# Scratch writes on SyncE's queue, later uses, single softmax steps and a fifth raw weight tile in a decoder trunk

## The chip, the core and the metric

The kernel runs on one core of one Trainium2 chip. The core has TensorE (PE, the matmuls), VectorE (DVE), ScalarE (ACT), GpSimd (POOL) and SyncE (SP), which here only issues transfers; sixteen DMA engines move data between the chip's DRAM and the core's memory. The metric is the device time of one execution in microseconds (us).

## The reference, cut to what matters

Four decoder layers with three kinds of token mixer in turn (layer 0 and 3: latent attention, layer 1: sparse attention with an indexer, layer 2: a window of 128 tokens with sinks), one row of 256 tokens, width 2048, all in float32. Every layer has one input projection, four memory cross-attention heads, a SiLU gate and one output projection:

```
def reference(x, mem, norm_in, final_norm, mem_norm, rel_bias, w_in_a, ...):
    mem_n = _rmsnorm(mem, mem_norm)
    for i in range(DEPTH):
        h = _rmsnorm(x, norm_in[i])
        kind, j = i % N_MIXERS, i // N_MIXERS
        if kind == 0:
            self_out, mq, gate = _mla_branch(h, w_in_a[j], a_q_norm[j], w_uq[j], a_kv_norm[j], w_ukv[j])
        elif kind == 1:
            self_out, mq, gate = _dsa_branch(h, w_in_b[j], rel_bias)
        else:
            self_out, mq, gate = _swa_branch(h, w_in_c[j], c_sinks[j], rel_bias)
        mem_out = _memory_attention(mq, mem_n @ w_mem_kv[i])
        y = jnp.concatenate([self_out, mem_out], axis=-1) * jax.nn.silu(gate)
        x = x + y @ w_out[i]
    return _rmsnorm(x, final_norm)
```

The latent branch makes queries from a compressed `c_q` (1536 wide, normed) and keys and values from `c_kv` (512 wide, normed); the other two have 32 heads of 64 over 4 key groups, with a relative position bias.

## The kernel before

**Weights.** Each matrix product is done as three float32r products, with activations and weights each cut into a high and a low part. A weight tile of two row tiles (`stage`, 512 KB, buffer `wr`, WR = 4 of them) is loaded on SP's queue; for each of the two, ACT copies the high part (`wh`, L75) and DVE subtracts (`wl`, L84), with WS = 4 buffers each; then PE runs six matmuls of 512 columns (`rows_by`, L381). Undisturbed that is 1.36 us for one row tile and 2.72 us for a stage; one row tile of 128 rows is called a k-tile below. The program is one long run of such stages.

**The scratch round trip.** An activation that is needed in the other layout goes through DRAM. DVE transposes blocks of the accumulator (`turn_blocks`, L284, tile `et`, or `z` first), `put` (L299) writes `et` to a scratch tensor `turned`, and `get` (L306) reads it back with four transfers into `fa` (the compressed streams), `fq` (queries), `kn` (keys), `pT` (softmax weights) or `gT` (gates). All of these are issued from GpSimd, in its program order. Then ACT cuts the tile into its parts, and DVE does the low ones: `gained` (`fa` to `cT`), `row_parts` (`fq` to `fq`), `exact_parts` (`kn`, `pT`), and the query parts of a key group, `qS`. A group's `pT` goes to PE's `o` (L1197) as it is.

**What sets the order.** `other_work` is called once for each stage: `tick` counts stages, and `after(n, job)` puts a job in n stages later. A read is put in BACK = 3 stages behind its write, a use USE = 9 stages behind it. A scheduler then sets the order on each engine from the program's order and its own model of durations; what is pinned (`keep_in_program_order`) stays in program order. So on ACT a use stands between the `wh` copies of later weights, and ACT takes its queue in order.

**The parts.** `Latent`, `Memory` and `GroupedPart` each work one slice of heads: queries, then softmax steps (`weights`, put in as jobs), then `weighted`, then the gate (`write`, `yt`, `y`). In a `GroupedPart` four softmax steps (half, odd) are put in at stages 1, 3, 5 and 7 behind `queries`, each with two `quarter_softmax`, and the bias tile `bm` is loaded at the part's start. In the last layer `split_ahead` cuts a piece of the last output weights ahead of time: 16 pieces of 256 columns, each loaded to `hl` (L1332), cut by ACT (L1342) and DVE (L1343) and written to scratch `sw` (L1346), pinned, on GpSimd's queue, two `hl` tiles in turn.

## Time and profile before

| | us |
|---|---|
| median of 3 runs | 2554.52 (2554.26 to 2557.95) |
| the profiled execution | 2558.04 |
| its span on the core | 2556.1 |
| PE busy | 2498.3 (98%) |
| DVE busy | 1853.7 (73%) |
| ACT busy | 1520.6 (59%) |
| POOL busy | 569.1 (22%) |

Engines' shares are of the span. A row of the timeline gives the start, the busy time, engine, line, operation, output and input tile, shape, how many in a row, and in brackets how long the engine was idle before and what ended that. A row of the waits gives, for one kind of instruction and one releaser, the idle time in total, how many times, and the longest. A row of the windows gives, for a stretch of the span, its length and then each engine's busy time, the granted TensorE clock as a share of its full speed, the share of the DMA engines and GB/s. A DMA issue row gives what is moved, whose queue, how many, the size and the median time from issue to landing.

### The profile page before, as it was taken

Reading aid. Unit: us, or ns where it says so; the run is one execution under the profiler, and the core shown is the slowest. Engines: PE = TensorE matmul, PEld = TensorE weight load, DVE = VectorE, ACT = ScalarE, POOL = GpSimd, SP = SyncE. Lnnn points to the kernel's source line nnn. Section 1 sums busy time; section 2 is a strip of 40 time slices with the busy share of each in tenths; the row PEclk is TensorE's granted clock in tenths of the full one; section 3 lists DMA queues with packets and bytes.
Section 4 is the critical chain, followed back from the end, with each engine's and each line's share of the span. In section 5 each row is a group of like instructions: output and inputs, shape, how many; then the busy total and the mean of one; then the engine's idle time right before and its main releaser. Section 6 shows DMA issues by size and latency. Waiting matters only on the chain. (4 is left out here: it accounts for less than half of the span.)

```text
span 2556.1 us, 37640 instructions
## 1 busy us (share of the span) xinstructions
PE 2498.3 (98%) x11766; PEld 2070.6 (81%) x11766; DVE 1853.7 (73%) x3840; ACT 1520.6 (59%) x3107; POOL 569.1 (22%) x1078
## 2 busy tenths in 40 slices
PE   9999999999999999999999999999999999999998
PEld 7888887787787889887878788878779778888887
DVE  6556555676776687887887776888867567777677
ACT  6555555565565557665666565666656555566564
POOL 3000001133222310123322112222320123432240
PEclk9999999999999999999999999999999999999999
DMA  8787767898879776778878677877875789997994
GB/s 283 250 267 236 235 213 227 233 259 238 228 233 264 236 243 203 222 225 255 276 234 246 200 222 245 253 246 246 245 238 173 224 248 278 267 263 225 269 313 148
DMA packets 404633, 613.96 MB, mean 240 GB/s; under 512 B 80881, under 2 KB 182641, under 8 KB 403793
## 3 DMA queue, kind: packets, MB, share of 16 engines
q1 hardware_dynamic: 347360, 449.71, 58.4%
q0 software_dynamic: 56352, 160.87, 20.3%
q8 instruction: 93, 1.52, 0.2%
q14 instruction: 108, 0.88, 0.1%
q10 hardware_dynamic: 720, 0.98, 0.1%
HBM read 535.83 MB, written 81.89 MB: 242 GB/s over the span
## 5 line engine op out<-in xcount | busy, mean ns | idle before, releaser
L75 ACT ACTIVATE wh<-wr 128x512 fp32r<-128x512 f32 (+1 forms) x1712 | 1046.5, 620 | 774.5 <-DVE wl L84 308.4
L84 DVE TENSOR_TENSOR wl<-wr,wh 128x512 fp32r<-128x512 f32 (+1 forms) x1712 | 1137.8, 676 | 482.7 <-ACT wh L75 473.2
L381 PE MATMUL acc_g<-wh,xT 128*128 128x512 f32 x1536 | 490.6, 394 | 5.3 <-ACT wh L75 5.3
L381 PE MATMUL acc_wo<-wh,y 128*128 128x512 f32 x1504 | 478.5, 393 | 3.6 <-ACT wh L75 3.4
L381 PEld LDWEIGHTS acc_g<-wh,xT 128*128 128x128 f32 x1536 | 290.7, 189 | 67.3 <-ACT wh L75 9.2
L381 PEld LDWEIGHTS acc_wo<-wh,y 128*128 128x128 f32 x1504 | 283.9, 189 | 62.5 <-ACT wh L75 5.6
L381 PE MATMUL acc_g<-wl,xT 128*128 128x512 f32 x768 | 304.6, 397 | 9.1 <-DVE wl L84 8.8
L381 PE MATMUL acc_wo<-wl,y 128*128 128x512 f32 x752 | 296.3, 394 | 2.2 <-DVE wl L84 2.0
L306 POOL DMA_DIRECT2D pT<-turned x320 | 175.0, 554 | 254.2 <-DMA turned<-et 43.1
L299 POOL DMA_DIRECT2D turned<-et x136 | 76.0, 559 | 549.7 <-DVE et L284 482.0
L381 PEld LDWEIGHTS acc_g<-wl,xT 128*128 128x128 f32 x768 | 145.4, 189 | 45.2 <-DVE wl L84 16.1
L381 PEld LDWEIGHTS acc_wo<-wl,y 128*128 128x128 f32 x752 | 142.2, 189 | 32.1 <-DVE wl L84 4.8
L381 PE MATMUL acc_mq<-wh,xT 128*128 128x512 f32 x512 | 162.6, 391 | 0.0
L381 PE MATMUL acc_mk<-wh,mT 128*128 128x512 f32 x512 | 160.4, 392 | 2.2 <-ACT wh L75 2.2
L381 PE MATMUL acc_q<-wh,xT 128*128 128x512 f32 x512 | 159.9, 390 | 0.0
L381 PE MATMUL acc_mv<-wh,mT 128*128 128x512 f32 x512 | 156.4, 389 | 0.9 <-ACT wh L75 0.9
L381 PE MATMUL acc_cq<-wh,xT 128*128 128x512 f32 x384 | 123.9, 402 | 6.4 <-ACT wh L75 6.4
L381 PE MATMUL acc_qn<-wh,cT 128*128 128x512 f32 x384 | 121.4, 392 | 3.5 <-ACT wh L75 3.2
L1367 DVE TENSOR_TENSOR xc<-xc,acc_wo 128x1024 f32<-128x1024 f32 x92 | 111.8, 1215 | 9.0 <-PE acc_wo L381 8.7
L381 PEld LDWEIGHTS acc_mk<-wh,mT 128*128 128x128 f32 x512 | 96.8, 189 | 22.8 <-ACT wh L75 2.6
L381 PEld LDWEIGHTS acc_mv<-wh,mT 128*128 128x128 f32 x512 | 96.0, 188 | 21.1 <-ACT wh L75 1.0
L381 PEld LDWEIGHTS acc_mq<-wh,xT 128*128 128x128 f32 x512 | 96.1, 188 | 19.8 <-ACT wh L75 0.7
(313 smaller groups left out, 3914.4 us busy)
## 6 DMA issues: line engine op xcount, KB each, us to landing
wr<-in_w_out_dram SPq DMA_DIRECT2D x188, 512.0 KB, 4.6
wr<-in_w_in_a_dram SPq DMA_DIRECT2D x176, 512.0 KB, 5.1
wr<-in_w_mem_kv_dram SPq DMA_DIRECT2D x125, 512.0 KB, 4.7
wr<-in_w_in_b_dram SPq DMA_DIRECT2D x116, 512.0 KB, 5.1
wr<-in_w_in_c_dram SPq DMA_DIRECT2D x104, 512.0 KB, 5.1
wr<-in_w_uq_dram SPq DMA_DIRECT2D x144, 256.0 KB, 5.3
turned<-et POOLq DMA_DIRECT2D x104, 256.0 KB, 4.4
wr<-in_w_ukv_dram SPq DMA_DIRECT2D x64, 256.0 KB, 6.0
```

The costliest lines, as they stand in the source:

```text
L75: inst = nc.scalar.activation(o, i, AF.Copy, scale=scale)
L84: nc.vector.tensor_sub(lo, src, f32(hi))
L299: nc.gpsimd.dma_start(d[t].rearrange("i p j n -> (i p) (j n)"), et)
L306: inst = nc.gpsimd.dma_start(dst[32 * j:32 * j + 32].rearrange("p (i n) -> p i n", n=n), d[:, :, :, j, :].rearrange("t i p n -> p (t i) n"))
L381: nc.tensor.matmul(acc[t][:, :n], q[:, v, (s + k) % 4, t * P:(t + 1) * P], w_[:, :n], start=s + k == 0 and v == 0 and w_ is wh, stop=s + k ...
L1367: nc.vector.tensor_add(xs, xs, acc)
```

## The change

1. `put` issues on SP's queue, where the weight loads are, instead of GpSimd's; `get` stays on GpSimd.
2. WR goes from 4 to 5: five raw weight tiles instead of four.
3. USE goes from 9 to 10 stages; for `weighted` there is WAIT = 9; the keys of the memory wait 6 stages as before, by a number of their own.
4. `row_parts` works in two halves, the second a stage later; a group's query parts `qS` are done in two steps, a stage apart; a memory part's second softmax comes 1 stage earlier in its second half (`part` 1).
5. A group's four softmax steps become eight single ones at stages 1, 3, ... 15; its bias load is put in 11 stages later; a memset of `e0` goes from GpSimd to DVE.
6. `split_ahead` takes 32 pieces of 128 columns instead of 16 of 256, each with half the stages between its steps; there are still two `hl` tiles, of half the size. The other users of the old `hl` tile get a `tmp` one.

```diff
--- before.py
+++ after.py
@@ -25,8 +25,8 @@
 MEMW = 1024
 ST = 2
 N_TAB = 384
-PQ, AUX, WR, WS, PT, WARM = 3, 4, 4, 4, 4, 11
-BACK, USE = 3, 9
+PQ, AUX, WR, WS, PT, WARM = 3, 4, 5, 4, 4, 11
+BACK, USE, WAIT = 3, 10, 9


 def _buckets():
@@ -68,8 +68,6 @@
     def f32(ap):
         return ap.bitcast(F32)

-    def part_tile(dt=F32R):
-        return wk.tile([P, 512], dt, name="hl", tag="hl", bufs=2)

     def copy_act(o, i, scale=1.0):
         inst = nc.scalar.activation(o, i, AF.Copy, scale=scale)
@@ -296,7 +294,7 @@
         if d is None:
             d = dr.tile([u, 4, 32, 4, n], F32, name="turned", tag=f"turned{u * n}", bufs=6)
         for t, et in enumerate(ets):
-            nc.gpsimd.dma_start(d[t].rearrange("i p j n -> (i p) (j n)"), et)
+            nc.sync.dma_start(d[t].rearrange("i p j n -> (i p) (j n)"), et)
         return d

     def get(dst, d, pin=None):
@@ -344,8 +342,12 @@
         hi, lo = (act.tile([P, 4, S], F32R, name="fq", tag="pq", bufs=PQ) for v in range(2))
         src = t.rearrange("p u m c -> p m u c")
         h4, l4 = (z.rearrange("p m (u c) -> p m u c", c=32) for z in (hi, lo))
-        copy_act(h4, src)
-        nc.vector.tensor_sub(l4, src, f32(h4))
+
+        def half(m):
+            copy_act(h4[:, m:m + 2], src[:, m:m + 2])
+            nc.vector.tensor_sub(l4[:, m:m + 2], src[:, m:m + 2], f32(h4)[:, m:m + 2])
+        half(0)
+        after(1, lambda: half(2))
         return hi, lo

     def exact_parts(hi, lo):
@@ -704,14 +706,14 @@
                         pin(inst)
                 self.k = act.tile([P, 2, 8, 4, 32], F32R, name="kn", tag="kn", bufs=1)
                 get(flat_of(self.k[:, 1]), mk[i][part], pin)
-                after(USE - BACK, lambda: exact_parts(self.k[:, 0], self.k[:, 1]))
+                after(6, lambda: exact_parts(self.k[:, 0], self.k[:, 1]))
             after(BACK if part == 0 else 11, keys)
             acc = rows_by(nm.at, 16, w, 0, (mq0 + part * 512, 512), "mq")

             def queries(t):
                 self.q = row_parts(t)
                 for h in range(2):
-                    after(1 + 2 * h, lambda h=h: self.weights(h))
+                    after(1 + (2 - part) * h, lambda h=h: self.weights(h))
             features(from_rows(acc), pq_tile, queries)
             gate(nm, w, g0 + 2048 + part * 512, self)

@@ -748,7 +750,7 @@
             def back():
                 pL = weights_tile()[:, :512]
                 get(f32(pL), d)
-                after(USE - BACK, lambda: self.weighted(h, pL))
+                after(WAIT - BACK, lambda: self.weighted(h, pL))
             after(BACK, back)

         def weighted(self, h, pL):
@@ -918,7 +920,7 @@
             def back():
                 pT = weights_tile()
                 get(f32(pT)[:, :384], d)
-                after(USE - BACK, lambda: self.weighted(h, pT))
+                after(WAIT - BACK, lambda: self.weighted(h, pT))
             after(BACK, back)

         def weighted(self, h, pT):
@@ -979,7 +981,7 @@
             s3 = src.rearrange("p (g d) -> p g d", g=n)
             for g0 in range(0, n, 2):
                 m = min(2, n - g0)
-                hl = part_tile()[:].rearrange("p (g v e d) -> p g v e d", g=2, v=2, e=2)
+                hl = tmp("hl", dt=F32R)[:].rearrange("p (g v e d) -> p g v e d", g=2, v=2, e=2)
                 for d in range(2):
                     split(hl[:, :m, 0, d, :], hl[:, :m, 1, d, :], s3[:, g0:g0 + m])
                 transposed(lambda i0, i1: dst(2 * g0 + i0, 2 * g0 + i1),
@@ -1092,16 +1094,19 @@
         def __init__(self, of, g):
             super().__init__()
             self.of, self.g, nm = of, g, of.nm
-            self.bm = bm = act.tile([P, 8, S], F32, name="bm", tag="big3")
             tab = tabs[0 if of.sparse else 1][g]
-            for v in range(2):
-                for e in range(2):
-                    at = 64 * v + 32 * e
-                    nc.gpsimd.dma_start(
-                        bm[at:at + 32, :4],
-                        bass.AP(tensor=tab.tensor,
-                                offset=tab.offset + 4 * e * N_TAB + 63 + 32 * v * (8 * N_TAB - 1),
-                                ap=[[8 * N_TAB - 1, 32], [N_TAB, 4], [1, S]]))
+
+            def biases():
+                self.bm = act.tile([P, 8, S], F32, name="bm", tag="big3")
+                for v in range(2):
+                    for e in range(2):
+                        at = 64 * v + 32 * e
+                        nc.gpsimd.dma_start(
+                            self.bm[at:at + 32, :4],
+                            bass.AP(tensor=tab.tensor,
+                                    offset=tab.offset + 4 * e * N_TAB + 63 + 32 * v * (8 * N_TAB - 1),
+                                    ap=[[8 * N_TAB - 1, 32], [N_TAB, 4], [1, S]]))
+            after(11, biases)
             acc = rows_by(nm.at, 16, of.w, 0, (g * 512, 512), "q")
             ets = []
             for t in range(2):
@@ -1111,22 +1116,25 @@

             def queries(t):
                 self.q = [act.tile([P, 2, 8, 2, 32], F32R, name="qS", tag="pq", bufs=PQ) for z in range(2)]
-                for z in range(2):
+
+                def parts(z):
                     for h, main, low in ((0, slice(0, 64), slice(64, P)), (1, slice(64, P), slice(0, 64))):
                         hi, lo = (self.q[z][rows, h].rearrange("p u j c -> p u (j c)") for rows in (main, low))
                         src = t[main, :, 2 * z:2 * z + 2, :].rearrange("p u j c -> p u (j c)")
                         copy_act(hi, src)
                         nc.vector.tensor_sub(lo, src, f32(hi))
+                parts(0)
+                after(1, lambda: parts(1))
                 while steps:
                     advance()
                 self.pTs = {}
                 self.ets = act.tile([P, 3, 640], F32, name="ets", tag="big2")
-                for n in range(4):
-                    after(1 + 2 * n, lambda n=n: self.weights(n // 2, n % 2))
+                for n in range(8):
+                    after(1 + 2 * n, lambda n=n: self.weights(n // 4, n // 2 % 2, n % 2))
             features(put(ets), pq_tile, queries)
             gate(nm, of.w, of.g0 + g * 512, self)

-        def weights(self, half, odd):
+        def weights(self, half, odd, second):
             of, g, bm, q = self.of, self.g, self.bm, self.q

             def score(r, k0, n):
@@ -1151,20 +1159,25 @@
             flat_et = self.ets[:, (2 * half + odd) % 3]
             et = flat_et.rearrange("p (j m c) -> p j m c", j=4, m=5)
             if of.sparse:
-                e2, e1 = bm[:, 4 + half * 2 + odd, :], ring(P)
-                quarter_softmax(score, bias, ((0, 0, e2[:, 192:]), (1, 0, e1)), None)
-                turn_blocks(et, 0, e1)
+                e2 = bm[:, 4 + half * 2 + odd, :]
+                if not second:
+                    e1 = ring(P)
+                    quarter_softmax(score, bias, ((0, 0, e2[:, 192:]), (1, 0, e1)), None)
+                    turn_blocks(et, 0, e1)
+                    return
                 e3 = ring(S)
                 quarter_softmax(score, bias, ((2, 0, e2[:, :192]), (3, 0, e3)), None)
                 turn_blocks(et, 1, e2, 2)
                 turn_blocks(et, 2, e3, 2)
             else:
                 nsk = nsink[:, u0:u0 + 1]
-                e0, e1 = ring(P), ring(P)
-                nc.gpsimd.memset(e0[:, 64:], 0.0)
-                quarter_softmax(score, bias, ((0, 0, e0[:, :64]), (1, 0, e1)), nsk)
-                turn_blocks(et, 0, e0)
-                turn_blocks(et, 1, e1)
+                if not second:
+                    e0, e1 = ring(P), ring(P)
+                    nc.vector.memset(e0[:, 64:], 0.0)
+                    quarter_softmax(score, bias, ((0, 0, e0[:, :64]), (1, 0, e1)), nsk)
+                    turn_blocks(et, 0, e0)
+                    turn_blocks(et, 1, e1)
+                    return
                 e2 = bm[:, 4 + 2 * odd:6 + 2 * odd, :].rearrange("p a b -> p (a b)")
                 quarter_softmax(score, bias, ((2, 0, e2[:, :192]), (3, 64, e2[:, 192:384])), nsk)
                 turn_blocks(et, 2, e2[:, :3 * P])
@@ -1175,7 +1188,7 @@
                 self.pTs[half, odd] = pT
                 get(flat_of(pT), d)
                 if len(self.pTs) == 4:
-                    after(USE - BACK, self.weighted)
+                    after(WAIT - BACK, self.weighted)
             after(BACK, back)

         def weighted(self):
@@ -1327,24 +1340,26 @@
         pin = tc.keep_in_program_order

         def load(n):
-            q = part_tile()[:].rearrange("p (v c) -> p v c", v=2)
-            k, c0 = part * 4 + n // 2 % 4, 1024 + n // 8 * 512 + n % 2 * S
-            pin(nc.gpsimd.dma_start(f32(q)[:, 1, :], w[k * P:(k + 1) * P, c0:c0 + S]))
+            q = wk.tile([P, 2, P], F32R, name="hl", tag="hl", bufs=2)
+            m = n // 2
+            k, c0 = part * 4 + m // 2 % 4, 1024 + m // 8 * 512 + m % 2 * S + n % 2 * P
+            pin(nc.gpsimd.dma_start(f32(q)[:, 1, :], w[k * P:(k + 1) * P, c0:c0 + P]))
             return q

         ahead = load(0)
         for _ in range(8):
             yield True
-        for n in range(16):
+        for n in range(32):
             q = ahead
-            if n < 15:
+            if n < 31:
                 ahead = load(n + 1)
             pin(nc.scalar.activation(q[:, 0, :], f32(q)[:, 1, :], AF.Copy))
             pin(nc.vector.tensor_sub(q[:, 1, :], f32(q)[:, 1, :], f32(q)[:, 0, :]))
-            for _ in range(4):
+            for _ in range(2):
                 yield True
-            pin(nc.gpsimd.dma_start(split_w[n // 4][:, n % 4], q))
-            for _ in range(6):
+            m, c0 = n // 2, n % 2 * P
+            pin(nc.gpsimd.dma_start(split_w[m // 4][:, m % 4, :, c0:c0 + P], q))
+            for _ in range(3):
                 yield True
```

How the change moves the instructions is seen in the order on the engines (what stands there in a row, with no time in it). ACT, layer 0, second latent slice, where the queries `fq` are cut between weight copies `wh`; before:

```order
L75 ACTIVATE y<-yt 128x512
L75 ACTIVATE wh<-wr 128x512 x2
L75 ACTIVATE vf<-acc_va 128x512
L75 ACTIVATE va<-acc_va 128x512
L75 ACTIVATE wh<-wr 128x512 x5
L75 ACTIVATE fq<-fq 128x1024
L75 ACTIVATE wh<-wr 128x512 x4
L650 ACTIVATE e,sm<-u,ms,qsn 128x128
```

and after:

```order
L73 ACTIVATE y<-yt 128x512
L73 ACTIVATE wh<-wr 128x512 x2
L73 ACTIVATE vf<-acc_va 128x512
L73 ACTIVATE va<-acc_va 128x512
L73 ACTIVATE wh<-wr 128x512 x3
L73 ACTIVATE fq<-fq 128x512
L73 ACTIVATE wh<-wr 128x512
L73 ACTIVATE fq<-fq 128x512
L73 ACTIVATE wh<-wr 128x512 x3
L652 ACTIVATE e,sm<-u,ms,qsn 128x128
```

The use stands two copies earlier, in two halves: five copies stood between `va` and `fq`, now three and four. Counted in k-tiles on each engine, from the last transpose on DVE to the first use on ACT, the places before and after are: `cT` 9, 11, 10, 10 and now 8, 9, 9, 9 (twice); `fq` 8 to 13 and now 7 to 10 in all but two of its sixteen; `qS` 9, 9, 9, 9, 8, 6, 5, 5 and now 5, 6, 6, 6, 5, 6, 6, 7. From the last transpose to a group's `o` on PE it was 16 to 20 and is 26 to 30.

GpSimd in the first and second key group of layer 1 (`pT`, `fq`, `gT` are reads of scratch; `turned` is a write; `bm` the bias load); before:

```order
L306 DMA pT_11997<-turned 32x4x160 x4
L299 DMA turned<-ets 128x640
L306 DMA pT_12102<-turned 32x4x160 x4
L1100 DMA bm<-tab_108 32x4x256 x4
L299 DMA turned<-ets 128x640
L299 DMA turned<-et 128x512
L306 DMA pT_12151<-turned 32x4x160 x4
L299 DMA turned<-et 128x512
L306 DMA fq<-turned 32x8x128 x4
L299 DMA turned<-th 128x512
```

and after:

```order
L304 DMA pT_11952<-turned 32x4x160 x4
L304 DMA pT_12096<-turned 32x4x160 x4
L304 DMA pT_12238<-turned 32x4x160 x4
L1104 DMA bm<-tab_108 32x4x256 x4
L304 DMA pT_12380<-turned 32x4x160 x4
L304 DMA fq<-turned 32x8x128 x4
L304 DMA gT<-turned 32x8x128 x4
```

The second write of `et` stood behind a read of `pT`; now GpSimd has reads alone. GpSimd, start of the last layer's `split_ahead`; before:

```order
L1332 DMA hl<-in_w_out_dram 128x256
L1346 DMA sw_131<-hl 128x512
L299 DMA turned<-et 128x512 x2
L1332 DMA hl<-in_w_out_dram 128x256
L306 DMA fq<-turned 32x8x128 x4
L1346 DMA sw_131<-hl 128x512
L1332 DMA hl<-in_w_out_dram 128x256
```

and after:

```order
L1346 DMA hl<-in_w_out_dram 128x128
L1361 DMA sw_131<-hl 128x2x128
L1346 DMA hl<-in_w_out_dram 128x128
L1361 DMA sw_131<-hl 128x2x128
L1346 DMA hl<-in_w_out_dram 128x128
L304 DMA fq<-turned 32x8x128 x4
L1361 DMA sw_131<-hl 128x2x128
L1346 DMA hl<-in_w_out_dram 128x128
```

There are twice as many pieces between the same reads. The 32 stand on ACT at 2 to 10 k-tiles from each other, mostly 2 to 5 (before 8 to 17). On SP the writes stand between the weight loads; a load stands there 8 k-tiles ahead of its first use (before 6).

## Rows read from the trace of the kernel before

**Rows 1.** The page: busy time of each engine.

```profile
PE 2498.3 (98%) x11766; PEld 2070.6 (81%) x11766; DVE 1853.7 (73%) x3840; ACT 1520.6 (59%) x3107; POOL 569.1 (22%) x1078
```

**Rows 2.** Waits of PE: instruction, releaser, us in total, times, longest.

```profile
PE acc_g L381 <- DVE wl L84: 8.8, 16, 1.6
PE acc_cq L381 <- ACT wh L75: 6.4, 3, 3.2
...
PE o L1197 <- DMA pT<-turned: 1.9, 1, 1.9
```

**Rows 3.** Waits of ACT, in the same columns.

```profile
ACT fq L75 <- DMA fq<-turned: 38.8, 12, 6.2
...
ACT qS L75 <- DMA fq<-turned: 24.8, 11, 6.5
ACT wh L75 <- DMA wr<-in_w_in_a_dram: 22.7, 14, 3.0
...
ACT cT L75 <- DMA fa<-turned: 18.5, 6, 4.5
```

**Rows 4.** Windows of 64 us: one stretch of layer 1.

```profile
1152.00:1216.00 64.00, 59.70 (x272) 47.96 (x271) 47.49 (x117) 35.17 (x78) 18.38 (x33) 0.97 0.83 251
```

**Rows 5.** Timeline 1186 to 1213 us, DVE, POOL, ACT, PE in turn.

```profile
1187.78 0.70 DVE L284 STREAM_TRANSPOSE et<-z 128x512 f32<-128x512 f32 x1
...
1191.88 2.20 POOL L306 DMA_DIRECT2D pT<-turned  x4 [4.39 <-PE acc_g L381]
1194.08 0.56 POOL L299 DMA_DIRECT2D turned<-et  x1
...
1205.39 1.15 ACT L75 ACTIVATE qS<-fq 64x512 fp32r<-64x512 f32 x2 [6.51 <-DMA fq<-turned]
...
1209.46 0.50 PE L381 MATMUL acc_g<-wh,xT 128*128 128x512 f32 x1 [1.45 <-ACT wh L75]
1211.61 0.50 PE L381 MATMUL acc_g<-wl,xT 128*128 128x512 f32 x1 [1.65 <-DVE wl L84]
```

**Rows 6.** Timeline 1726 to 1745 us, DVE and ACT, a group of layer 2.

```profile
1732.48 0.70 DVE L284 STREAM_TRANSPOSE et<-z 128x512 f32<-128x512 f32 x1
...
1741.64 1.15 ACT L75 ACTIVATE qS<-fq 64x512 fp32r<-64x512 f32 x2 [0.46 <-DMA fq<-turned]
```

**Rows 7.** Timeline 811 to 831 us, POOL and ACT, second latent slice.

```profile
812.58 1.16 POOL L299 DMA_DIRECT2D turned<-et  x2 [10.97 <-DVE et L284]
818.47 2.34 POOL L306 DMA_DIRECT2D fq<-turned  x4 [4.73 <-DMA turned<-et]
...
828.24 1.06 ACT L75 ACTIVATE fq<-fq 128x1024 fp32r<-128x1024 f32 x1 [5.57 <-DMA fq<-turned]
```

**Rows 8.** Timeline 1376 to 1412 us, DVE, POOL, ACT, PE: memory queries, layer 1.

```profile
1387.39 1.27 DVE L284 STREAM_TRANSPOSE et<-acc_mq 128x512 f32<-128x512 f32 x2
...
1391.83 1.11 POOL L299 DMA_DIRECT2D turned<-et  x2
...
1408.91 1.06 ACT L75 ACTIVATE fq<-fq 128x1024 fp32r<-128x1024 f32 x1 [5.42 <-DMA fq<-turned]
...
1410.54 0.77 PE L381 MATMUL acc_wo<-wh,y 128*128 128x512 f32 x1 [2.28 <-ACT wh L75]
```

**Rows 9.** The page: DMA issues.

```profile
wr<-in_w_in_a_dram SPq DMA_DIRECT2D x176, 512.0 KB, 5.1
...
turned<-et POOLq DMA_DIRECT2D x104, 256.0 KB, 4.4
...
wr<-in_w_in_a_dram SPq DMA_DIRECT2D x32, 288.0 KB, 3.2
```

**Rows 10.** Tile `hl`: POOL's idle before it (us, times), and landing times.

```profile
  DMA sw<-hl: 15.4, 4
...
DMA to landing us min/median/max: 2.9/6.1/8.6
```

## The prediction

> **What bounds the kernel now.** I read the page's busy line first. PE is busy 98% of a span of 2556.1 us [rows 1], so there are 2556.1 − 2498.3 = 57.8 us of idle time to win, and what the clock gives back. The matrix work itself isn't touched by the change. Second, the waits of PE [rows 2]: it waits for split weights, `wh` from ACT or `wl` from DVE, 1 to 3 us at a time. ACT is busy only 59%, so it can't be its work. Third, therefore, the waits of ACT [rows 3]: its long ones are at a use of scratch (`fq` 38.8 us in 12, `qS` 24.8 in 11, `cT` 18.5 in 6), where the reads haven't landed; ACT stands there in order, with the next weight copies behind. A weight load is waited for more often than long (at most 3.0 us).
>
> The timelines show how such a wait reaches PE. ACT idles 6.51 us at `qS`, PE 1.45 + 1.65 = 3.10 [rows 5]; ACT 5.42 at `fq`, PE 2.28 [rows 8]. The differences, 3.4 and 3.1, are the lead that ACT has over PE. So I work with **PE's stall = ACT's idle − 3.3 us**, nothing below that. A stall can also cost clock: in the 64 us around the stall of rows 5 the granted clock is 0.97 [rows 4], that is part of the stretch at 1.2 instead of 2.4 GHz, worth some 0.03 x 64 = 1.9 us.
>
> So the question is, for each use, whether its reads land sooner (queue), and whether the use stands earlier or later on ACT (order). The change's "ten stages" suggests later. The order on ACT says the opposite: most uses stand 1 to 4 k-tiles closer behind their transposes.
>
> **The change part by part.** The sum is made against the profiled 2558.0 us (3.5 above the median; 1.9 lie outside the span and stay).
>
> *Writes off GpSimd's queue, in the key groups.* The transpose ends at 1187.78 + 0.70 = 1188.48; its write is issued at 1194.08 only, behind a read of `pT` which waited 4.39 us for a tile that PE had to free [rows 5]. That is 5.6 us lost, and the chain to the landed reads is 1205.39 − 1188.48 = 16.9 us. In a group of layer 2, with no such queueing, it is 1741.64 − 1733.18 = 8.5 us [rows 6]. After the change GpSimd has reads alone there, so I take the short chain plus up to 3 us for slower landings: 8.5 to 11.5. ACT reached the use at 1205.39 − 6.51 = 1198.88, 10.4 us behind the transpose; standing 3 k-tiles of 1.36 us earlier, it gets there after 6.3 to 8. ACT's idle: 0.5 to 5, middle 2.8, below 3.3; I keep 0.6 of stall. That gives −2.5, −1.9 of clock, and −1.0 for the other groups of layer 1, whose idle is mostly under the lead (24.8 − 6.5 over ten waits is 1.8 each). **−5.4** (−9 to 0).
>
> *The same in the memory queries of layers 1 and 2.* Transposes end at 1387.39 + 1.27 = 1388.66, writes are issued at 1391.83 behind `pT` reads, 3.2 us late [rows 8]. But the use there goes from 13 to 9 k-tiles, which takes most of it back. I take half of the stall and half a clock loss: **−2.1** (−6 to +2).
>
> *The write itself on SP.* On GpSimd, from the first write's issue to the reads' issue it takes 818.47 − 812.58 = 5.9 us for two writes of 256 KB [rows 7], and one write lands in 4.4 [rows 9]. No row shows a scratch write on SP's queue amid the loads. Nearest: a load of 288 KB on it lands in 3.2, one of 512 KB (both writes together) in 5.1 [rows 9]. So between 2.7 us sooner (5.9 − 3.2) and, if both stand behind a whole load, 5.1 + 3.2 = 8.3, 2.4 later. I take 5.0, **0.9 us sooner**, nearest to the row of 512 KB, and use it in the next two terms.
>
> The Trainium skill's page "DMA: Bandwidth & Descriptors", section "Issuing engines are not separate DMA queues", speaks against this gain: transfers of all issuing engines run on the same 16 DMA engines, and another issuer saves only the time of issuing. By it the 0.9 would be about 0, and the sum below some 4 us higher; no run shown here has moved a write.
>
> *Latent and memory queries, uses nearer.* At 828.24 ACT idles 5.57 us [rows 7], a stall of some 2.2 by the rule. With the use 2 k-tiles earlier and the write 0.9 sooner: 5.57 + 2.7 − 0.9 = 7.4. `row_parts` in halves gives back half of a 1.06 us copy, so the stall is 3.6, 1.4 more. Three of the long `fq` waits in latent parts move so, others 0 or 1 k-tile and stay under the lead: 3 x 1.4 − 1.2 for those that don't move = **+3** (−3 to +12).
>
> *`cT`.* PE has 3 stalls there, 6.4 us [rows 2], out of six waits of ACT [rows 3]. 1 k-tile less, 0.9 sooner: 3 x (1.36 − 0.9) = **+1.4** (−5 to +6).
>
> *`o` of the groups* goes from 16 to 20 k-tiles behind its transposes to 26 to 30: the 1.9 us [rows 2] go, **−1.9**. The tiles `pT` are then held longer (four, as before); what waits for them are GpSimd's reads, and nothing else stands there that is short of time but the next group's query reads.
>
> *Eight softmax steps.* DVE does the same work (73% busy) in smaller lumps between the `wl`. PE's waits for `wl` sum to 8.8 us in 16 [rows 2], 1.65 of it counted above. A quarter of the rest: **−2** (−5 to 0). The memset (64 columns), the later bias load and the softmax spacing: nothing, since DVE is idle 27%.
>
> *Fifth raw tile.* Loads stand 8 instead of 6 k-tiles ahead. ACT's waits for loads, 22.7 us in 14 for the largest matrix [rows 3], are 1.6 each and below the lead, so alone they cost PE nothing; where they fall shortly ahead of a scratch use they eat the lead. **−4** (−8 to 0).
>
> *SP's queue* gets the 232 writes between its loads. A write waits for its transpose with loads behind it; but a load's buffer comes free by DVE too, and in DVE's order no load behind a write could have gone before it. **0** (0 to +6, if real order differs from the order in the program).
>
> *`split_ahead` in 32.* One piece's round through an `hl` tile is load 6.1 us (the median) + ACT and DVE, about 1 + write 6.1 = some 13 us [rows 10], and two tiles serve one piece in 6.6. Pieces now stand at 2 to 5 k-tiles, 2.7 to 6.8 us, for long stretches. ACT and DVE wait in order at the piece. GpSimd already waited 15.4 us in 4 for these writes [rows 10]. Halves land sooner (2.9 us is the shortest), which leaves 2 x 2.9 + 1 = 6.8 for two, 3.4 each. So between 0 and 20; **+3**, nearer the low end since ACT's lead of 3.3 covers most single waits.
>
> Sum: −5.4 − 2.1 + 3 + 1.4 − 1.9 − 2 − 4 + 0 + 3 = **−8.0**, 2558.0 − 8.0 = 2550.0 profiled, less 3.5 is **2546.5 on the median's scale**; own range 2538 to 2553.
>
> **The rivals.**
>
> *A larger gain.* The writes on SP land 2.7 us sooner, like the row of 288 KB. Then every chain is shorter by more than its use has moved (1 to 2 k-tiles, 1.4 to 2.7): the +3 and +1.4 go, with them the 6.4 of `cT`, some 6 of `fq` and three clock losses of 1.9. 2546.5 − 4.4 − 12.4 − 5.7 = **2524**. For it: SP writes nothing of its own, and GpSimd's issue of two writes alone takes 1.16 us [rows 7]. Against: loads keep that queue full.
>
> *No change.* Queue and order cancel: `fq` and `cT` at twice my cost (+4.4), and the two queue terms at half (+3.7): 2546.5 + 8.1 = **2555**. For it: the 13 to 9 k-tiles of rows 8, which is the very place of the queueing.
>
> *Slower.* The write stands behind weight loads on SP's queue, and the uses are nearer: ACT's `fq` and `cT` waits, 18 with 57.3 us, mean 3.2 [rows 3], sit right at the lead, so that each us later costs PE up to 18 us. With the write 1.5 us later than now and uses 1.36 us nearer, the mean is 6.0, 2.7 over the lead; 18 x 2.7 = 49 less what is already stalled there (6.4 and some 9) would be +33, and some 25 as a third of the waits are far below it. In place of +4.4, that is 2546.5 + 20.6 = **2567**. It decides from about half a us later than now. The Trainium skill's page "DMA: Bandwidth & Descriptors", section "Queues, rings and completion order", bears on it: it says that a DMA engine consumes a ring's descriptors in order and takes rings in turn; so a write on SP's ring would stand behind its loads, where on GpSimd's it took turns with them. No row here shows it.
>
> *Slower by `split_ahead`.* At its upper end of +20: 2546.5 + 17 = **2564**. It decides where a piece's round is over two pieces' distance on ACT, for the whole stretch.
>
> *That the change doesn't do what it says* is met above: uses at "ten stages" stand nearer, not further.
>
> **How the numbers follow.** My forecast 0.43, the larger gain 0.11, no change 0.22, slower by the queue 0.16, slower by `split_ahead` 0.08. What a measurement of this kernel can tell from none is about 0.2%, 5.1 us, so faster is under 2549.4, slower over 2559.6. Of the forecast's own 0.43, 0.35 lie under 2549.4 and 0.08 above. Faster 0.35 + 0.11 + some of the no-change case's lower part 0.04 = 0.50; same 0.08 + 0.18 = 0.26; slower 0.24. The range 2522 to 2567 leaves out half of the larger gain and half of the slower cases.
>
> **What would show it.** In the profile after: `turned<-et` on SP's queue at about 4 us (3.2 or less: the larger gain; over 5.5: slower). ACT's `qS` waits at most 3 us, PE with no stall near the groups' queries of layer 1, no wait at `o`. `fq` and `cT` waits as many and as long as now, or a little longer. ACT's waits for `wr` gone but for a few us. In the last layer, `hl` on ACT waiting for its load some us in total. I'm wrong where the scratch waits on ACT shrink as a whole (then writes on SP are faster than thought) or PE stalls at `hl`.

## The result and the profile after

The changed kernel takes 2592.1 us (median of four executions, 2581.6 to 2600.7) against 2554.6: ratio 1.014, interval 1.0098 to 1.0185. It is slower by 1.4%, some 38 us, where 8 us of gain were forecast, and lies above the range of 2522 to 2567.

The page of the changed kernel, profiled in an execution of 2586.89 us, busy time of each engine:

```profile
span 2585.1 us, 37748 instructions
...
PE 2512.0 (97%) x11766; PEld 2072.8 (80%) x11766; DVE 1857.7 (72%) x3888; ACT 1525.2 (59%) x3139; POOL 458.4 (18%) x862
```

Against [rows 1] the span is 29.0 us longer. PE's idle time in it is 2585.1 − 2512.0 = 73.1 in place of 57.8, which is 15.3 more, and the same 11,766 matmuls are busy 13.7 longer. GpSimd lost its writes (POOL some 111 us less), and this brought no gain in time. The waits of PE and of ACT in the changed kernel (instruction, releaser, us in total, times, longest):

```profile
PE acc_g L383 <- ACT wh L73: 10.3, 9, 2.9
PE acc_g L383 <- DVE wl L82: 10.2, 21, 0.9
PE sp L1143 <- DVE yt L1220: 6.4, 4, 1.8
...
PE acc_cq L383 <- ACT wh L73: 4.9, 6, 2.7
```

```profile
ACT fq L73 <- DMA fq<-turned: 50.1, 15, 7.1
ACT pT L73 <- DMA pT<-turned: 39.9, 27, 6.3
ACT qS L73 <- DMA fq<-turned: 34.1, 10, 6.0
ACT hl L1356 <- DMA hl<-in_w_out_dram: 33.9, 15, 5.7
...
ACT cT L73 <- DMA fa<-turned: 25.6, 8, 5.1
```

ACT's long waits for scratch have all grown [rows 3]: `fq` from 38.8 to 50.1, `qS` from 24.8 to 34.1, `cT` from 18.5 to 25.6, and `pT` from 26.3 to 39.9. A new one, 33.9 us, stands at the `hl` pieces. The waits for `wr` of the largest matrix are gone but for 2.8 us, as forecast. PE's waits for `wl` are a few more and shorter (21 times in place of 16, at most 0.9 us in place of 1.6), and those of `sp` behind `yt` are new.

The scratch writes themselves became faster. Those of 256 KB on the page:

```profile
turned<-et SPq DMA_DIRECT2D x104, 256.0 KB, 3.9
```

3.9 us in place of 4.4 [rows 9]. With the wait to be issued, the mean of all `et` writes from the end of the last transpose to the landing went from 5.7 to 4.2 us. The place of [rows 7], second latent slice, in the changed kernel shows both halves of the matter (timeline, DVE, SP's queue, POOL, ACT in turn):

```profile
808.75 1.31 DVE L282 STREAM_TRANSPOSE et<-acc_qn 128x512 f32<-128x512 f32 x2 [0.79 <-PE acc_qn L383]
809.49 0.94 SPq L297 DMA_DIRECT2D turned<-et  x2
...
813.93 1.16 POOL L304 DMA_DIRECT2D fq<-turned  x2 [17.67 <-DMA turned<-et]
...
820.59 0.63 ACT L73 ACTIVATE fq<-fq 128x512 fp32r<-128x512 f32 x1 [3.22 <-DMA fq<-turned]
```

The transposes end at 810.06 and the reads have landed at some 820.5: 10.5 us. That is a short chain. But ACT got to the use at 820.59 − 3.22 = 817.37, only 7.3 us behind the transposes, and stood there. Over all 16 `fq` places the timelines give: from the transposes to the landed reads 14.4 us before and 12.8 after (1.6 sooner), from the transposes until ACT is free for the use 12.3 before and 9.8 after (2.5 sooner). For the eight `cT` uses, 13.1 to 11.9 and 11.1 to 8.8.

### The profile page after: what moved, and what is told of

The parts are those of the page before. It is cut to its first block, busy times and chain, and to the rows that moved or that the text cites. A ratio compares the mean times of both kernels' runs of the same rounds, so it can differ in the third digit from the quotient of the medians.

```text
span 2585.1 us, 37748 instructions
## 1 busy us (share of the span) xinstructions
PE 2512.0 (97%) x11766; PEld 2072.8 (80%) x11766; DVE 1857.7 (72%) x3888; ACT 1525.2 (59%) x3139; POOL 458.4 (18%) x862
## 5 line engine op out<-in xcount | busy, mean ns | idle before, releaser
L383 PE MATMUL acc_g<-wl,xT 128*128 128x512 f32 x768 | 305.8, 398 | 10.2 <-DVE wl L82 10.2
L1382 DVE TENSOR_TENSOR xc<-xc,acc_wo 128x1024 f32<-128x1024 f32 x92 | 111.6, 1213 | 6.1 <-PE acc_wo L383 5.9
L304 POOL DMA_DIRECT2D fq<-turned x112 | 64.9, 587 | 286.6 <-DMA turned<-et 169.4
L383 PEld LDWEIGHTS acc_mk<-wh,mT 128*128 128x128 f32 x512 | 96.8, 189 | 22.3 <-ACT wh L73 2.1
```

What stands on the lines that cost most here:

```text
L304: inst = nc.gpsimd.dma_start(dst[32 * j:32 * j + 32].rearrange("p (i n) -> p i n", n=n), d[:, :, :, j, :].rearrange("t i p n -> p (t i) n"))
L383: nc.tensor.matmul(acc[t][:, :n], q[:, v, (s + k) % 4, t * P:(t + 1) * P], w_[:, :n], start=s + k == 0 and v == 0 and w_ is wh, stop=s + k ...
L1382: nc.vector.tensor_add(xs, xs, acc)
```

## The experiments

Theories, as the expectations name them. **1:** the 32 pieces of `split_ahead` cost some 20 us. **2:** the writes on SP with the uses nearer cost most of it; **2a:** because the uses stand too near, though the writes are no slower; **2b:** because writes and loads disturb each other on SP's queue. **3:** the fifth raw tile lets loads and uses stand nearer and so costs time. **4:** the eight softmax steps stretch a group, so that `sp` waits for `yt`. Names that begin with a are the changed kernel with an edit, those with b the kernel before. Ratios are to the kernel before as it ran beside them (medians 2555.9 to 2558.3).

### One part undone, or alone

**a_put_pool** takes only the writes back to GpSimd's queue; **b_put_sp** is the opposite, the writes alone in the kernel before.

```diff
-            nc.sync.dma_start(d[t].rearrange("i p j n -> (i p) (j n)"), et)
+            nc.gpsimd.dma_start(d[t].rearrange("i p j n -> (i p) (j n)"), et)
```

> The changed kernel with the scratch writes back on GpSimd's queue. Theory 2 (writes behind weight loads on SP's queue are what costs): 15 to 25 us faster, near 2570. Theory 1 (pieces): no faster in layers 0 to 2, and in the last layer worse or the same, since GpSimd's queue waits at hl with the scratch writes then behind it: 2595 to 2620.

Measured: 2540.7 us, 0.994 (0.992 to 0.996). This one line is worth 51 us in the changed kernel, twice what theory 2 asked for, and the rest of the change is a gain of 0.6%. Page and ACT's waits:

```profile
PE 2489.7 (98%) x11766; PEld 2067.2 (81%) x11766; DVE 1860.1 (73%) x3888; ACT 1529.3 (60%) x3139; POOL 589.9 (23%) x1094
```

```profile
ACT fq L73 <- DMA fq<-turned: 24.0, 11, 3.9
...
ACT cT L73 <- DMA fa<-turned: 18.5, 8, 3.6
```

`fq` waits for 24.0 instead of 50.1. The spans differ by 45.2 us: 22.9 of PE's idle time and 22.3 of busy time on the same matmuls.

Between these two kernels only the writes' queue differs, so their timelines compare the chain (from the transposes to the landed reads) with the room (from the transposes until ACT is free for the use):

| mean, us | chain, a_put_pool | chain, changed | room, a_put_pool | room, changed |
|---|---|---|---|---|
| `fq`, 16 places | 13.7 | 12.8 | 12.4 | 9.8 |
| `qS`, 8 | 14.2 | 12.0 | 10.1 | 6.2 |
| `cT`, 8 | 13.1 | 11.9 | 10.9 | 8.8 |
| `pT` of the latent layers, 32 | 13.7 | 11.1 | 15.2 | 11.1 |

With the writes on SP every chain is 1.0 to 2.6 us shorter, and every room 2.1 to 4.1 us.

> The kernel before with one edit: the scratch writes on SP's queue. Theory 2 in either form (this edit is what costs): 30 to 60 us slower than before, 2585 to 2615; the uses stand at 8.2 k-tiles for fq (before 10) and 4.2 for qS (before 7.5). The prediction's step (the write lands 0.9 us sooner, the nearer uses cost 4): about 2554, within 10 us.

Measured: 2587.7 us, 1.012 (1.007 to 1.016): the writes alone cost some 32 us, with no other part of the change. ACT's waits show the same picture:

```profile
ACT fq L75 <- DMA fq<-turned: 53.5, 16, 7.3
...
ACT cT L75 <- DMA fa<-turned: 33.4, 8, 5.3
```

USE is still 9 here, so it isn't the "ten stages". Theory 2 holds in both kernels. The weight loads don't suffer from the writes between them: ACT waits 68 us for `wr` here, 65 in the kernel before and 7 in the changed kernel.

**a_wr4** and **a_hl16_wr4**: four raw tiles again; and with them 16 pieces of 256 columns, as before (the `hl` tiles of double width need the room of the fifth).

```diff
-PQ, AUX, WR, WS, PT, WARM = 3, 4, 5, 4, 4, 11
+PQ, AUX, WR, WS, PT, WARM = 3, 4, 4, 4, 4, 11
...
-            q = wk.tile([P, 2, P], F32R, name="hl", tag="hl", bufs=2)
+            q = wk.tile([P, 2, S], F32R, name="hl", tag="hl", bufs=2)
...
-        for n in range(32):
+        for n in range(16):
```

> The changed kernel with four raw weight tiles instead of five, all else kept. Theory 1 (the pieces of split_ahead cost about 20 of the 30 to 38 us, in the last layer): the last layer costs as much as with five tiles. The prediction's step (the fifth tile is worth about 4 us): some 2596 us, with ACT's waits for wr back at 40 us or more. Theory 3 (the fifth tile lets the scheduler put uses nearer, and so costs): under 2585.

> The changed kernel with four raw weight tiles and the old split_ahead: 16 pieces of 256 columns with the old spacing (five raw tiles and the larger pieces don't fit together). To be read against the run with four tiles alone. Theory 1 (pieces): about 20 us less than that run, all of it in the last layer, POOL's wait for sw at hl from about 87 back to about 15 us. Theory 2 (writes on SP's queue and nearer uses cost it all): within 5 us of that run.

Measured: 2611.8 (1.020, 1.013 to 1.026) and 2599.0 (1.016, 1.012 to 1.020). Four tiles are 20 us slower than five (executions 2595 to 2623 against 2582 to 2601), so theory 3 falls: the fifth tile is a gain. At equal tiles the 32 pieces cost 13 us, some two thirds of what theory 1 has, and don't carry the 51.

**b_hl32** and **b_hl32_wr5**: the 32 pieces alone in the kernel before (with a `tmp` tile for the other users of `hl`), and with the fifth tile.

```diff
-        for n in range(16):
+        for n in range(32):
...
-PQ, AUX, WR, WS, PT, WARM = 3, 4, 4, 4, 4, 11
+PQ, AUX, WR, WS, PT, WARM = 3, 4, 5, 4, 4, 11
```

> The kernel before with one edit: split_ahead in 32 pieces of 128 columns. Against the same with a fifth raw tile (2552) it prices the tile, against before (2556) the pieces. If the pieces alone cost what they seemed to in the changed kernel: 2570 to 2580. The prediction's step (+3): 2559.

> The kernel before with two edits that need each other for space: 32 pieces of 128 columns in split_ahead and a fifth raw weight tile; writes stay on GpSimd. If the fifth tile is worth the 20 us that taking it away cost in the changed kernel, and the pieces cost 20: about 2555. The prediction's steps (-4 and +3): 2554. If pieces cost only where the writes are on SP (there ACT's pieces stand nearer each other): 2535 to 2545.

Measured: 2569.5 (1.0033, 1.0014 to 1.0053) and 2551.8 (0.9983, 0.9961 to 1.0005). The pieces cost 11 us here too, the tile gives 18 back. In the last layer ACT now waits for `hl` and GpSimd for the writes of the tile (b_hl32; ACT's waits, then tile `hl`: GpSimd's idle time, us and times):

```profile
ACT hl L1343 <- DMA hl<-in_w_out_dram: 20.6, 14, 4.3
```

```profile
  DMA sw<-hl: 52.1, 17
```

**a_steps4** and **b_steps8**: four double softmax steps in the changed kernel; eight single ones in the kernel before.

```diff
-                for n in range(8):
-                    after(1 + 2 * n, lambda n=n: self.weights(n // 4, n // 2 % 2, n % 2))
+                for n in range(4):
+                    after(1 + 2 * n, lambda n=n: self.weights(n // 2, n % 2))
```

> The changed kernel with the groups' softmaxes put in as four double steps again, at 1, 3, 5, 7. Theory 4 (the eight steps stretch a group's part so that o holds its accumulators and sp waits: PE waits 6.4 us for yt, layer 2 is some 10 us longer than before): 8 to 12 us faster, all in layers 1 and 2, no PE wait of sp on yt. Theories 1 and 2: within 5 us of the changed kernel.

> The kernel before with one edit: the groups' softmaxes as eight single steps. Theory 4 (the longer part makes sp wait for yt): 8 to 12 us slower than before. The prediction's step: 4 us faster, with no wait of PE at o.

Measured: 2580.5 (1.008, 1.005 to 1.011), 11.6 better than the changed kernel (its slowest execution, 2583.2, is just over the changed kernel's fastest, 2581.6); and 2561.4 (1.0023, 0.9998 to 1.0048), not told apart from none. The wait of theory 4 appears with the eight steps alone (b_steps8, PE):

```profile
PE sp L1135 <- DVE yt L1212: 3.9, 4, 2.2
...
PE acc_wo L381 <- ACT y L75: 3.2, 3, 1.5
```

In the changed kernel it looks like this (timeline, DVE and PE, end of a group in layer 1):

```profile
1216.99 0.69 DVE L1220 TENSOR_TENSOR yt<-o,gT 128x512 f32<-128x512 f32 x1 [1.80 <-DMA turned<-th]
1217.73 0.28 PEld L1143 LDWEIGHTS sp<-kd,qS 128*128 128x128 f32 x1 [2.35 <-DVE yt L1220]
1217.74 0.47 PE L1143 MATMUL sp<-kd,qS 128*128 128x128 f32 x1 [1.84 <-DVE yt L1220]
```

The group is now so long that `o` keeps its accumulators until `yt` of one group while the next group's `sp` wants them. Here `yt` had itself waited 1.80 us for the write of a gate tile. So theory 4 is right on the wait (6.4 us); as a price, 4 to 12 us, it is small beside the writes.

### Nearness or the queue

**a_slow** sets the 32 pieces further apart, seven half stages instead of five.

```diff
-            for _ in range(2):
+            for _ in range(3):
...
-            for _ in range(3):
+            for _ in range(4):
```

> The changed kernel with the 32 pieces of split_ahead spread: 7 half stages from piece to piece instead of 5, all else as changed. Theory 1 (the pieces' round through two tiles, load and write 4 to 5 us each, is longer than their distance on ACT): 12 to 20 us faster in the last layer, 2572 to 2580, POOL's wait at hl for sw from 87 to under 40 us and ACT's wait at hl from 34 to under 10. If the last layer is long for another reason: 2587 or more.

Measured: 2592.5 (1.016, 1.012 to 1.020): nothing won. GpSimd still waits 89.7 us in 22 for `sw` and ACT 26.7 in 12 for `hl`. The pieces did move apart on ACT, from 8.5 to 11.1 us in the mean, so at these distances it isn't their distance that costs.

**a_gate7** holds the uses in their place. DVE makes the scale that ACT's cut takes (1, or the gain) from the last `wl` ahead of stage 7 behind the write, so that no order can put the use ahead of this; values are unchanged. It holds `cT`, `fq`, `qS` and `qrT`. **a_gate_all** does it at stage 8, and holds `kn` of the latent layers (stage 7), `pT` (stage 6) and the `hl` pieces as well; **a_gate_all_slow** adds the edit of a_slow.

```diff
+    def hold(cell, gcol=None, n=1):
+        col = small("gc", 4, bufs=4)
+        w = f32(last[0])
...
+            nc.vector.tensor_scalar(col[:, :1], w[:, :1], 0.0, 1.0, op0=OP.mult, op1=OP.add)
...
+        after(7, lambda: hold(cell, gcol, 4))
...
-            copy_act(h4[:, m:m + 2], src[:, m:m + 2])
+            copy_act(h4[:, m:m + 2], src[:, m:m + 2], scale=gc)
```

> The changed kernel, writes on SP's queue, but each use of scratch on ACT (cT, fq, qS, qrT) takes its scale from a column that DVE writes with the weights of a stage seven behind the write, so that the use can't stand nearer. From the last transpose to the use there are now 10 k-tiles for fq (changed kernel 8.4, with the writes on GpSimd 10.2), 9.5 for cT (8.8, 10), 7.8 for qS (5.9, 8.6). Theory 2a (the uses stand too near, the writes themselves are not slower): 35 to 55 us faster than the changed kernel, 2535 to 2555, and ACT's idle at fq half or less. Theory 2b (writes and weight loads disturb each other on SP's queue): within 10 us of the changed kernel, about 2590.

> The changed kernel, writes on SP, with all uses on ACT held back by a column from DVE: fq at 12.2 k-tiles behind its transpose (10.2 with the writes on GpSimd, 8.4 in the changed kernel), cT 11, qS 9.8, kn 12.6, pT 13.1 (11.8 and 9.5). The 32 pieces of split_ahead stand on ACT where they stood. Holding back fq, cT and qS at 10, 9.5 and 7.8 brought layer 0 down by 8 us and nothing elsewhere. Theory 2a (uses too near, in layers 1 to 3 for qS, pT and kn): layers 0 to 2 as with the writes on GpSimd, 14 us below before at the end of layer 2; the last layer still 20 us longer by its pieces: 2555 to 2570. Theory 2b (loads and writes on one queue): layers 1 and 2 stay 25 us longer, over 2585.

> Both: writes on SP, all uses held back, pieces spread. Theories 1 and 2a together: all of the loss is undone and the writes that land 1.2 to 1.6 us sooner are left as a gain: 2530 to 2545. Theory 2b: 2570 or more.

Measured: 2596.3 (1.016, 1.012 to 1.019), 2576.6 (1.009, 1.006 to 1.013) and 2568.5 (1.0055, 1.003 to 1.008). a_gate7 cut `fq` from 50.1 to 18.6 us and won nothing as a whole: the loss went to `pT` (39.9 to 53.3), which wasn't held, and to PE's longer waits for `wh`:

```profile
PE acc_g L406 <- ACT wh L73: 28.4, 14, 5.9
```

In layer 0 alone it did in part what theory 2a says: at the start of the layer's last output product it stood 10.2 us ahead of the kernel before (a_put_pool 11.5, the changed kernel 1.8), at the first weight product of layer 1 still 6.5 (11.0 and 2.5). The edit of a_gate_all got back 16 of the 51 us, with the pieces spread 24. None of the three lies where 2a had it: a_gate7's time is that of 2b, the other two lie between the two theories. The hold isn't free either: in a_gate_all ACT is busy 22.5 us longer than in the changed kernel, DVE 17.3. In a_gate_all_slow little of what is left is in ACT's long waits (`fq` 4.6 us, though 16.0 for the memory keys, which aren't held). A wait of DVE has grown, of a transpose for the write of its own tile; a_gate_all_slow, then the changed kernel and a_put_pool:

```profile
DVE et L283 <- DMA turned<-et: 26.6, 11, 4.2
```

```profile
DVE et L282 <- DMA turned<-et: 11.8, 9, 1.8
```

```profile
DVE et L282 <- DMA turned<-et: 9.8, 9, 2.3
```

It was 1.6 us in 3 before. Since a_put_pool has nearly as much of it as the changed kernel, it isn't what parts those two; it is what grew where the uses are held. These transposes of softmax weights share one `et` tile. As I read it, the scheduler expects the write to be faster, so the next transpose is set close behind it, and `wl` waits behind that in DVE's order; the twins below give the numbers. 2a as I had it, uses on ACT alone, was too narrow.

**a_pool_extra** is a_put_pool with a second, unread write of every tile on SP's queue: the queue's load without the nearer order.

```diff
+            x = dr.tile([4, 32, 4, n], F32, name="spare", tag=f"extra{n}", bufs=6)
+            nc.sync.dma_start(x.rearrange("i p j n -> (i p) (j n)"), et)
```

> The changed kernel with the writes on GpSimd, and every written tile written a second time, on SP's queue, to a scratch that nobody reads (some 60 MB more traffic). SP's queue has the 232 writes among its loads, and the uses stand no nearer than with the writes on GpSimd (fq 12.2 k-tiles, cT 10.8, qS 9.8). Theory 2a: 2540 to 2560, the traffic alone costing a little. Theory 2b: 2575 or more, with long waits of ACT for wr and scratch.

Measured: 2586.4 (1.010, 1.007 to 1.012). It looks like 2b but can't be read so: it moves some 60 MB more, and all landings grew, the writes on GpSimd's queue to 5.6 us and the loads to 6.0, where the changed kernel has 3.9 and 5.2. Inconclusive.

### Versions with the writes' queue as before, and a twin

**a_pool_steps4** is a_put_pool with the four steps. **a_s4_some_sp** is the same with 96 of the 232 writes on SP (the gates', the groups' softmax weights and the memory keys).

```diff
-        d = put(ets)
+        d = put(ets, q=nc.sync)
```

> The changed kernel with two parts undone: writes on GpSimd's queue and four double softmax steps. If the two effects seen apart add (about 50 us and about 11 us less than the changed kernel): 2525 to 2533. If the four steps only help where uses stand near: 2540, like the writes on GpSimd alone. If the eight steps bring something once the writes are on GpSimd: over 2545.

> The changed kernel with four double softmax steps, and only those 96 of the 232 scratch writes on SP's queue whose readers have long slack (gates, groups' softmax weights, memory keys); the writes of fq, cT, kn, qS and of the latent and memory pT are on GpSimd. The uses on ACT stand where they stand with all writes on GpSimd (fq 10.3 k-tiles, cT 10, pT 11.5). Theory 2a (it is the place of the uses): 2528 to 2545, like all writes on GpSimd (2537). Theory 2b (writes and weight loads on one queue disturb each other): about 40% of the way to all on SP (2580), 2553 or more.

Measured: 2536.5 (0.9925, 0.990 to 0.995) and 2543.3 (0.995, 0.993 to 0.998). These 96 writes are no gain on SP either; the executions of the two overlap. The time is in the range of 2a and under the 2553 of 2b.

**a_pool_s4_gate** is a_pool_steps4 with `cT`, `fq`, `qS` and `qrT` held at stage 8; **a_sp_s4_gate** is its twin with all writes on SP; **b_gate8** is the hold alone in the kernel before. The held uses stand at the same places in the twins (`fq` 12.2 and 12.1 k-tiles behind the transposes). From the twin on GpSimd to the one on SP:

```diff
-            nc.gpsimd.dma_start(d[t].rearrange("i p j n -> (i p) (j n)"), et)
+            nc.sync.dma_start(d[t].rearrange("i p j n -> (i p) (j n)"), et)
```

> The changed kernel with writes on GpSimd, four double softmax steps, and the uses of fq, cT and qS held back by DVE's column to 12, 11 and 9.5 k-tiles (10.6, 10 and 6.9 without). Theory 2a says that ACT's idle at these uses costs PE wherever the room is shorter than the chain: 5 to 15 us faster than without the holding back (2537), 2522 to 2532. If the places no longer matter: 2537.

> The twin of the kernel with writes on GpSimd, four double steps and fq, cT and qS held back (2527.9 us): the same but for all writes on SP's queue. The held uses stand alike (fq 12.2 k-tiles here, 12.1 there; cT 11 and 11.2; qS 9.8 and 9.5); pT and kn, not held, stand nearer here (10.0 against 12.0, 11.6 against 13.9). Theory 2a for fq, cT and qS alone: 2525 to 2540. Theory 2a with pT and kn as its rest: 2540 to 2560, with ACT's waits at pT and kn the longest. Theory 2b: over 2565, with waits that no place of a use explains.

> The kernel before with its uses of fq, cT and qS held back and nothing else: from 10 k-tiles to 12.4 for fq, 10 to 11.2 for cT, 7.5 to 9.5 for qS. Theory 2a in its simplest form (in the kernel before, too, the room is shorter than the chain: 12.3 against 14.4 us for fq, 11.1 against 13.1 for cT): 8 to 18 us faster than before, 2538 to 2548. If place doesn't decide: 2553 to 2560.

Measured: 2527.9 (0.988, 0.985 to 0.991), 2562.6 (1.0026, 1.0006 to 1.0046) and 2542.7 (0.994, 0.992 to 0.996). The hold alone gives 0.6% to the kernel before, where uses had been set too near as well, and a_pool_s4_gate beats both kernels by 1.2% and more. The twins are 35 us apart, and the one on SP, at 2562.6, lies between what 2a (up to 2560) and 2b (over 2565) had for it. Waits of the twin on SP, then of the one on GpSimd:

```profile
DVE et L283 <- DMA turned<-et: 27.3, 11, 4.8
...
ACT pT L73 <- DMA pT<-turned: 49.0, 19, 7.4
...
ACT fq L73 <- DMA fq<-turned: 3.7, 3, 3.0
```

```profile
DVE et L283 <- DMA turned<-et: 0.3, 1, 0.3
...
ACT pT L73 <- DMA pT<-turned: 30.8, 20, 4.2
...
ACT fq L73 <- DMA fq<-turned: 14.2, 5, 4.9
```

Where the uses are held, SP's writes are the better ones (`fq` 3.7 against 14.2 us). The longer waits are at what wasn't held and came nearer: `pT` (10.0 k-tiles behind its transposes in place of 12.0) and the next transpose. At the eleven places where a transpose stood in the twin on SP, the write had landed 6.3 us behind its transposes in the mean, in the other twin 8.3; but DVE was free for the next transpose 3.9 us behind them in place of 9.6. So 2.0 us were won and 5.7 lost. These writes were also slower than most of their kind: had each landed at the median of the softmax writes, 4.2 us, 7.7 of the 27.3 would be left. For `pT` the means alone don't explain the longer waits: at the 32 latent places the chain is 2.7 us shorter (14.0 to 11.3) and the room 1.9 (15.6 to 13.7). One of the eleven places, timeline of the twin on SP, SP's queue, DVE and PE:

```profile
596.28 0.34 SPq L298 DMA_DIRECT2D turned<-et  x1
...
604.11 0.31 DVE L283 STREAM_TRANSPOSE et<-e 128x128 f32<-128x128 f32 x1 [4.82 <-DMA turned<-et]
...
605.05 0.69 PE L406 MATMUL acc_wo<-wl,y 128*128 128x512 f32 x1 [2.02 <-DVE wl L83]
```

This write took 604.11 − 596.28 = 7.8 us where the median of its size (192 KB) is 4.1; the transpose stood for it, and PE for `wl` behind. Windows of these times, the twin on SP and the one on GpSimd, which is 9.7 us further on in the program at the start and 14.0 at the end (length, then busy time and count of PE, PEld, DVE, ACT and POOL; clock, DMA share, GB/s):

```profile
600.00:632.00 32.00, 29.98 (x132) 24.32 (x130) 19.07 (x30) 14.38 (x25) 6.64 (x12) 0.95 0.82 231
```

```profile
600.00:632.00 32.00, 32.00 (x149) 26.60 (x148) 21.75 (x34) 17.62 (x30) 9.10 (x16) 1.00 0.92 267
```

So 2 us of stall and 0.05 x 32 = 1.6 of clock, of the 4.3 that the twin on SP fell behind here. Summed over the span, ACT's idle time at scratch and pieces beyond 3.3 us each is 14.0 and 7.6 in the twins, 6 apart, and PE's idle time 61 and 38, 24 apart: most of what parts the twins doesn't go through ACT's long waits.

**What stays open.** The chains on SP aren't longer as a whole (`fq` 12.7 against 14.2 us in the twins), which speaks against 2b as the main cause. So does the place of the loss: the twin on SP falls behind by 24.8 us up to the first weight product of layer 1 and by 23.6 in layer 3, and gains 5.0 and 2.9 in layers 1 and 2, though the writes stand among the loads in all four. The latent layers 0 and 3 have all of the unheld `kn` that is read from a fresh write, and most of the `pT`. (That is one execution of each; between executions of kernels with the same code for layer 0, the changed kernel and a_steps4, this place differs by 6.5 us.) But some of 2b is there: the reads for `cT`, also in these layers, land in 7.3 us behind SP's writes and 5.7 behind GpSimd's (the last of four, in the twins), and single writes on SP took up to 10.7 us (8.5 before), which a median doesn't show. How much of the 35 us is nearness and how much such late writes isn't separated, and the hold, as a way to separate them, brought back less than 2a asked for; a kernel with its writes on SP and exactly the order of the GpSimd one wasn't made.

## Why the prediction was wrong

**The write on SP, right.** Forecast 0.9 us sooner, from the first of two writes' issue to both landed. At the `fq` places this is 5.7 us before and 5.0 in the changed kernel; by the one line alone it is 0.3 (b_put_sp) to 0.5 sooner. The rest of the 1.5 us is the wait to be issued. The rival "slower" had the write later by 1.5, which is refuted, though the time went past its 2567; its other half, uses nearer at waits that sit right at the lead, is what happened. The "larger gain" asked for 2.7 sooner, which wasn't reached.

**Uses nearer: the step that failed.** I had the order in hand, saw uses 1 to 4 k-tiles nearer, and priced this as a cost only for `fq`, +3, and `cT`, +1.4, with most of it paid by the faster write; in the two queue terms I set it off against the shorter chain. Measured, `fq` room fell by 2.5 us and the chain by 1.6, over 16 places. The terms of writes and uses (−5.4, −2.1, +3, +1.4, 0, together −3.1) measured **+51** in the changed kernel and +32 alone. What I left out: `pT` and `kn` on ACT (26.3 to 39.9 and 13.0 to 19.3 us of waits), and DVE's next transpose into a tile that is still being written, which follow the same forecast of the write. How the 51 us divide among these waits isn't shown. I asked where the use of each read stands, and should have asked what else waits for the same write.

**The grouped queue and the memory queries.** The queueing went as forecast: the wait to be issued for a group's query write fell from 2.0 us on average to nothing, and the chain from 14.2 to 12.0, just over my 8.5 to 11.5. ACT's `qS` waits still grew, to 6.0 at the longest where I had at most 3, since the uses followed (7.5 to 5.9 k-tiles). The −5.4 was no gain.

**PE's stall by ACT's idle less 3.3 us.** As a sum it held for the changed kernel: ACT's idle beyond 3.3 us each went from 20.1 to 31.6, 11.5 more, PE's idle time 15.3 more; in a_put_pool 13.0, 7.1 less, and PE 7.6 less. It doesn't hold elsewhere: in b_put_sp the rule gives 8.2 more than before and PE is idle 18.6 more, and in a_gate_all, where waits go through DVE, ACT has 8.8 left and PE is idle for 68.7 us, 10.9 more than in the kernel before. So that the sum held in the two kernels is in part luck.

**Clock.** I gave each stall 1.9 us and counted a handful. In the changed kernel against a_put_pool the matmuls are busy 22.3 us longer, as much as the idle time. The granted clock's mean, 0.989 against 0.994, explains 2585.1 x 0.011 − 2539.9 x 0.006 = 13 of that; for the other 9 I have no row. One stretch of the last layer, the changed kernel, then a_put_pool, which at these times is 25 to 35 us further on in the program (columns as above):

```profile
2140.00:2204.00 64.00, 59.47 (x268) 48.24 (x267) 45.95 (x108) 38.76 (x87) 23.65 (x40) 0.95 0.80 227
```

```profile
2140.00:2204.00 64.00, 64.00 (x306) 53.69 (x305) 49.23 (x112) 40.72 (x87) 29.16 (x50) 1.00 0.95 271
```

**`o` and the eight steps.** The `o` wait went as forecast, and came back as `sp` behind `yt` (6.4 us) and `acc_wo` behind `y` (3.1). −1.9 and −2 were in fact +4 (writes on GpSimd; two medians that overlap) to +12.

**Fifth raw tile.** −4 forecast, −18 and −20 measured. Waits for loads below the lead do cost: with four tiles the lead is gone when the next scratch wait comes. The last of this is argued from the waits, not shown by a run of its own.

**32 pieces.** +3 forecast, +11 and +13 measured; the round through the `hl` tile is seen on the timeline of the changed kernel (POOL and ACT):

```profile
2150.28 0.72 POOL L1361 DMA_DIRECT2D sw<-hl  x1
...
2155.55 0.31 ACT L1356 ACTIVATE hl<-hl 128x128 fp32r<-128x128 f32 x1 [5.73 <-DMA hl<-in_w_out_dram]
...
2157.61 0.57 POOL L1346 DMA_DIRECT2D hl<-in_w_out_dram  x1 [6.62 <-DMA sw<-hl]
```

ACT stands 5.73 us, and PE 1.89 behind it. I took 2.9 us, the shortest landing, for the halves; the medians are 3.6 (loads) and 5.0 (writes), so with 1 us for ACT and DVE a round is 9.6 us, and two tiles serve one piece in 4.8 where I had 3.4. The middle of my 0 to 20 would have been right, but since spreading the pieces won nothing (a_slow), by what they cost stays open.

**Sum.** +51 for the writes, +4 for the steps, −18 for the tile, +11 for the pieces, and −11 left for the halves, the stages of the other uses and the later bias load, by difference alone: +37. With the +32 of the kernel before in place of +51 the rest would be +8, so it is no measurement. That the change "doesn't do what it says" was the rival that came nearest, and I gave it no price.

## What to carry to other kernels

When a transfer becomes faster in a scheduler's own model, list everything that waits for it, consumers and the next writer of its buffer, and read from both orders how much nearer each was set; what counts is the room that is lost, less the time that is won. A use that has to stay late must be held by a dependency, since a count of stages in the program doesn't hold it. And price a tile of prefetch by a run: its own waits, all under the lead, said 4 us here where 18 to 20 were measured.

## What the runs showed of the hardware

By the one line alone (b_put_sp against the kernel before, the changed kernel against a_put_pool), a scratch write waits 0.1 us in the mean to be issued on SP's queue amid the weight loads, where it waited 1.0 and 0.9 on GpSimd's, and one of 256 KB lands in 4.1 us in place of 4.4 and in 3.9 in place of 4.1 (medians). Of the 1.4 and 1.0 us that a write is through sooner, 0.9 and 0.8 are the wait to be issued. The Trainium skill, "DMA: Bandwidth & Descriptors", section "Issuing engines are not separate DMA queues", says that another issuer saves issue time only; the trace agrees for the larger part.

The slowest single writes are slower on SP's queue: 10.0 and 10.7 us, where GpSimd's took 8.5 and 8.8. Halving a piece doesn't halve its landing: the load of 64 KB to `hl` lands in 3.6 us and its write of 128 KB in 5.0, where the double sizes took 5.0 and 6.8 (medians; over both 4.3 in place of the 6.1 of [rows 10]).
